# Moving the activations of a decoder layer by 64 bytes against its weights in SBUF

## The chip, the core and the metric

The kernel runs on one core of a Trainium2 chip. The metric is the device time of one execution in microseconds, the median of three runs. The five engines are named as in the profile: PE (TensorE) with its weight loads as PEld, DVE (VectorE), ACT (ScalarE), POOL (GpSimd) and SP (SyncE), which issues nearly all loads.

## The reference, cut to what matters

One decoder layer for 256 tokens of width 1024, all in float32:

```python
h = rmsnorm(x, norm1_g)
proj = h @ w_in                       # q, k/v, gates, MoBA q/k/v, merge gates
y_nsa, y_moba = nsa_attention(...), moba_attention(...)
mixed = g_nsa * (y_nsa @ w_up_nsa) + g_moba * (y_moba @ w_up_moba)
x = x + mixed @ w_out
u = relu(rmsnorm(x, norm2_g) @ w_ff1)
x = x + (u * u) @ w_ff2
return rmsnorm(x, norm_f_g)
```

## The kernel before, in words

Weights come as 60 chunks of up to 128 x 2048 float32 (1 MB), one after the other, through three buffers `raw`. The function `split` (L102) makes two float32r tiles of each chunk: ACT copies it, rounded, to `whi`, and DVE subtracts to give the remainder `wlo`. Activations are split in the same way, into tiles whose names end in h and l. A product of two split operands is three matmuls, high by high, high by low and low by high (`mm3`, L240); nearly every matmul of the kernel goes through the helper `mm` (L237), so the profile shows one line for them and tells them apart by their tiles. Each matmul loads its stationary operand (128 columns, an LDWEIGHTS in the row PEld) and then streams its moving operand. In a name such as `acc<-whi,hTh` the moving operand stands first and the stationary one second.

There are two kinds of these products:

- **Activations stationary, weights moving.** `xstat` (L245) for the input projections with h^T (tiles `hTh`, `hTl`); the products of the attention outputs y^T (`yTh`, `yTl`) with the up-projections (loop at L731); `ff2_mms` (L955) for the second feed-forward product with the squared activations (`sqh`, `sql`); and `seven_mms` (L968), which multiplies six of the sixteen chunks of `ff2` with seven block products instead of eight, its stationary blocks being squared activations or sums of them (`sh`, `sl`, and `sxh`, `sxl` for the sixth), its moving ones weights or differences of weights (`th`, `tl`). The moving operand has 512 columns, except in the first four chunks (384 or 408 columns) and in the last 24 matmuls (256).
- **Weights stationary, activations moving.** `wstat` (L260), with 256 moving columns, for `mixed @ w_out` (tiles `mxh`, `mxl`) and for the first feed-forward product (tiles `h2h`, `h2l`).

The order of the work is written out by hand. `run_slot` (L223) issues the matmuls of one chunk and puts in between, at given shares of the list, the splitting of the chunk after next, the load of a later one, and the steps of the attention. The kernel schedules nothing by itself; the tiles' places in SBUF come from the order in which they are allocated, and unused tiles called `gap...` shift what follows. `act_pair` (L186) makes the pair of tiles that hold h^T first, the mixed activations later, and in the end the sums for the seven products; its argument is the element at which the operand begins in its tile, so the two users can begin at different places of one buffer.

What this case is about is where a partition's bytes of an operand begin, modulo 256. As the built program before has them, in bytes:

| operand | begins at, modulo 256 | past the weights |
|---|---|---|
| `raw`, `whi`, `wlo`, `th`, `tl` | 128 | 0 |
| h^T | 128 | 0 |
| y^T | 128 | 0 |
| squared activations | 128 | 0 |
| sums for the seven products | 128 | 0 |
| mixed activations, `h2h`, `h2l` | 64 | 192 |

All slices of these operands that a matmul takes start a multiple of 256 bytes further, so the table holds for every matmul, with one exception: in the two chunks `kvb` the weights' four blocks have 408 columns, 1632 bytes, so block k begins 1632 k bytes on: 0, 96, 192 and 32 bytes past the first, modulo 256.

Of the kernel before, what the change touches and what calls it, by code (L numbers as in the profile page):

```python
# [8 lines left out]
F32 = mybir.dt.float32  # L9
# [32 lines left out]
def hybrid_layer(ctx: ExitStack, tc: tile.TileContext, firstd, gxd, w, w1c, small, const, gf, out):  # L42
# [8 lines left out]
    ap_ = at_stack.enter_context(tc.tile_pool(name="att", bufs=1))  # L51
# [134 lines left out]
    def act_pair(name, o):  # L186
        return (cp.tile([128, 2048 + e], F32R, name=name + n, tag="act" + n.upper())[:, o:o + 2048]
                .rearrange("p (k q) -> p k q", k=8) for n, e in (("h", 128), ("l", 16)))

    hTh, hTl = act_pair("hT", 16)  # L190

    def h_part(kt):
        x = x0[:, kt, :] if kt < 4 else xT[:, kt, :]
# [266 lines left out]
        act.activation(pcT, tp[:, 0:256], AF.Copy)  # L460


    yTh = {m: ap_.tile([128, 4, 256], F32R, name=f"yTh{m}") for m in "nm"}
    yTl = {m: ap_.tile([128, 4, 256], F32R, name=f"yTl{m}") for m in "nm"}

    PAIRS = [[("n", p, 1), ("n", p, 2)] for p in range(4)] + [
        [("m", p, 0), ("m", p + 1, 0)] for p in (0, 2)]
# [310 lines left out]
    FB = {}  # L778

    def open_ff():  # L780
        at_stack.close()
        FB["p"] = ctx.enter_context(tc.tile_pool(name="ff", bufs=1))
        FB["o"] = ctx.enter_context(tc.tile_pool(name="ps_o", bufs=1, space=PS))
        p = FB["p"]
        p.tile([128, 48], F32, name="gap")
        for n in "hl":
            FB["h2" + n] = (p.tile([128, 2176 if n == "h" else 2096], F32R, name="h2" + n, tag="h2" + n)[:, 48:2096]
                            .rearrange("p (k q) -> p k q", k=8))
        p.tile([128, 80], F32, name="gap2")
        FB["sqh"] = p.tile([128, 32, 256], F32R, name="sqh")  # L790
        FB["sql"] = p.tile([128, 32, 256], F32R, name="sql")
        FB["gfb"] = p.tile([128, 1024], F32, name="gfb")
        FB["x1"] = p.tile([128, 2, 1024], F32, name="x1")
        FB["scr"] = p.tile([128, 1024], F32, name="fscr")
        FB["fst"] = p.tile([128, 24], F32, name="fst")
# [28 lines left out]
    for i in range(4):  # L824
        c = C_WOUT + i
        if i == 0:
            at(0.03, lambda: mix_t(0, 1, bank("yb", "yb")))
            at(0.04, mix_l, 0, 1)
            at(0.29, lambda: mix_t(1, 1, s_tile(1)[:, 0]))
            at(0.3, mix_l, 1, 1)  # L830
            lo_late(0.35, c - 1)
        elif i == 1:
            lo_late(0.03, c - 1)
        split_events(c, (0.0, 0.1), ((9, 9), (0.3, 0.3), (0.3, 0.3), (9, 9))[i])
        for f, a in prev:
            at(0.02, f, *a)
        if i == 1:
            at(0.01, open_ff)
            at(0.9, lambda: act.dma_start(FB["gfb"], gf[None, :].to_broadcast([128, 1024])))
        if i == 3:  # L840
            outs = [acc_tile()[:, 0:256] for _ in range(2)]
            at(0.52, wout_evac, i, outs, (0,))
            run_slot([m for j in range(2)
                      for m in wstat(outs[j], c, j * 128, 8, 256, mxh, mxl)])
            prev = [(wout_evac, (i, outs, (1,)))]
        else:
            mms, outs, _ = two_blocks(c, mxh, mxl, 4 if i == 0 else 8)
            run_slot(mms)
            prev = [(wout_evac, (i, outs))]
# [9 lines left out]
    SS, TT = {}, {}  # L859
# [5 lines left out]

    def s_sums(i, r):
        if not SS:
            FB["p"].tile([128, 40], F32, name="gap3")
            for n, e in (("h", 128), ("l", 16)):
                SS[n] = cp.tile([128, 2048 + e], F32R, name="s" + n, tag="act" + n.upper())  # L870
                SS[n + "x"] = FB["p"].tile([128, 384], F32R, name="sx" + n)
        j = SEVEN.index(i)
        for n in "hl":
            SS[i, n] = (SS[n][:, 16 + 384 * j:400 + 384 * j] if j < 5 else SS[n + "x"])
        S = [FB["scr"][:, 128 * a:128 * a + 128] for a in range(4)]
        A = [[r[:, k, 128 * t:128 * t + 128] for k in range(2)] for t in range(2)]
        for o, x, y, op in ((0, A[1][0], A[1][1], ALU.add), (2, A[0][0], A[1][0], ALU.subtract),
                            (1, S[0], A[0][0], ALU.subtract), (3, A[0][1], S[1], ALU.subtract)):
            dve.tensor_tensor(S[o], x, y, op=op)
# [26 lines left out]
    def ff1_evac(i, outs, whole):  # L906
        r = FB["p"].tile([128, 2, 256], F32, name="ur", bufs=2)
        rf = r.rearrange("p a q -> p (a q)")
        h, l = (FB[n][:, 2 * i:2 * i + 2, :].rearrange("p a q -> p (a q)") for n in ("sqh", "sql"))
        if whole is None:  # L910
            for m in range(2):
                act.activation(r[:, m], outs[m], AF.Relu)
        else:
            act.activation(rf, whole, AF.Relu)
        dve.tensor_tensor(rf, rf, rf, op=ALU.mult)
        act.activation(h, rf, AF.Copy)  # L916
        dve.tensor_tensor(l, rf, h.bitcast(F32), op=ALU.subtract)  # L917
        if i in SEVEN:
            s_sums(i, r)
# [252 lines left out]
```

## Time and profile before

| | |
|---|---|
| median of three runs | 377.09 us (375.64, 377.78, 377.09) |
| span of the profiled execution | 374.1 us |
| PE busy, PEld busy | 365.5 us (98%), 320.9 us (86%) |
| DVE busy, ACT busy | 294.9 us (79%), 219.9 us (59%) |
| matmuls, and as many weight loads | 2388 |
| bytes moved by DMA | 66.89 MB, mean 179 GB/s |
| mean granted TensorE clock | 0.997 |

The page gives no time of the profiled execution other than its span. The three timed runs are 1.5 to 3.7 us above that span, the median 3.0 us; this is what lies around the instructions. The durations of matmuls in the trace overlap, since a matmul's record reaches to the modelled end of its drain. What a matmul takes away from the next is the distance between two starts, and that is what is read below. The stages follow each other in the span: input projections with h^T to about 146 us, with the attention in between; up-projections with y^T from 146 to 173, with the end of the attention in between; `mixed @ w_out` and the first feed-forward product from 173 to 283; the second feed-forward product from 283 to 368; the last sums and stores.

### The profile page before, as it was taken

Reading aid. Unit: us, or ns where it says so; the run is one execution under the profiler, and the core shown is the slowest. Engines: PE = TensorE matmul, PEld = TensorE weight load, DVE = VectorE, ACT = ScalarE, POOL = GpSimd, SP = SyncE. Lnnn points to the kernel's source line nnn. Section 1 sums busy time; section 2 is a strip of 40 time slices with the busy share of each in tenths; the row PEclk is TensorE's granted clock in tenths of the full one; section 3 lists DMA queues with packets and bytes.
Section 4 is the critical chain, followed back from the end, with each engine's and each line's share of the span. In section 5 each row is a group of like instructions: output and inputs, shape, how many; then the busy total and the mean of one; then the engine's idle time right before and its main releaser. Section 6 shows DMA issues by size and latency. Waiting matters only on the chain.

```text
span 374.1 us, 6002 instructions
## 1 busy us (share of the span) xinstructions
PE 365.5 (98%) x2388; PEld 320.9 (86%) x2388; DVE 294.9 (79%) x476; ACT 219.9 (59%) x383; POOL 6.1 (2%) x18
## 2 busy tenths in 40 slices
PE   8999999999999999999999999999999999999993
PEld 7987778878888788778999999999998888888883
DVE  4878888896966869766867688787778879999685
ACT  6966465767747667344455566666664785555412
POOL 2020000000000000000000000000000000000000
PEclk9999999999999999999999999999999999999998
DMA  8996445334533335550675556556655535655202
GB/s 278 366 380 249 142 182 197 112 114 127 189 135 115 112 122 192 155 207 1 223 286 190 185 190 217 156 191 226 209 153 201 203 136 163 231 199 207 100 0 112
DMA packets 10539, 66.89 MB, mean 179 GB/s; under 512 B 1168, under 2 KB 1680, under 8 KB 3216
## 3 DMA queue, kind: packets, MB, share of 16 engines
q1 hardware_dynamic: 10080, 65.61, 50.1%
q10 hardware_dynamic: 432, 0.92, 0.6%
q8 instruction: 18, 0.29, 0.3%
q14 instruction: 9, 0.07, 0.1%
HBM read 65.47 MB, written 1.05 MB: 178 GB/s over the span
## 4 chain that ended last, share of the span: by engine, by line
PE 83%; DVE 7%; ACT 4%; DMA 3%; issue 2%; POOL 1%; SPq 0%; POOLq 0%; ACTq 0%; DVEq 0%
PE acc L238 53%; PE o L238 13%; PE P L238 4%; PE qacc L238 3%; PE yb L238 2%; DVE wlo L116 2%; ACT whi L114 2%; DMA raw<-in_kva_dram 2%; DMA g0x<-in_first_dram 1%; DVE x L988 1%; PE Sa L529 1%; PE Sb L529 1%; PE Sa L238 1%; PE Sb L238 1%; PE tp L319 1%
## 5 line engine op out<-in xcount | busy, mean ns | idle before, releaser
L114 ACT ACTIVATE whi<-raw 128x1024 fp32r<-128x1024 f32 (+3 forms) x124 | 118.4, 984 | 53.2 <-PE acc L238 33.7
L116 DVE TENSOR_TENSOR wlo<-raw,whi 128x1024 fp32r<-128x1024 f32 (+3 forms) x124 | 136.2, 1130 | 13.6 <-ACT whi L114 13.5
L238 PE MATMUL acc<-h2h,whi 128*128 128x256 f32 x256 | 70.7, 276 | 0.0
L238 PE MATMUL acc<-h2l,whi 128*128 128x256 f32 x256 | 70.7, 276 | 0.0
L238 PE MATMUL acc<-h2h,wlo 128*128 128x256 f32 x256 | 70.7, 276 | 0.0
L238 PE MATMUL acc<-whi,hTh 128*128 128x512 f32 (+1 forms) x128 | 51.0, 399 | 0.2 <-DVE kml L338 0.2
L238 PE MATMUL acc<-wlo,hTh 128*128 128x512 f32 (+1 forms) x128 | 50.7, 396 | 0.0
L238 PE MATMUL acc<-whi,hTl 128*128 128x512 f32 (+1 forms) x128 | 49.7, 388 | 0.0
L238 PEld LDWEIGHTS acc<-h2h,whi 128*128 128x128 f32 x256 | 48.0, 188 | 0.0
L238 PEld LDWEIGHTS acc<-h2l,whi 128*128 128x128 f32 x256 | 48.0, 188 | 0.0
L238 PEld LDWEIGHTS acc<-h2h,wlo 128*128 128x128 f32 x256 | 48.0, 188 | 0.0
L238 PE MATMUL o<-whi,sqh 128*128 128x512 f32 (+1 forms) x86 | 33.1, 385 | 0.0
L238 PE MATMUL o<-whi,sql 128*128 128x512 f32 (+1 forms) x86 | 33.0, 384 | 0.0
L238 PE MATMUL o<-wlo,sqh 128*128 128x512 f32 (+1 forms) x86 | 33.0, 384 | 0.0
L238 PEld LDWEIGHTS acc<-whi,hTh 128*128 128x128 f32 x128 | 24.3, 190 | 6.6 <-issue 1.3
L238 PEld LDWEIGHTS acc<-whi,hTl 128*128 128x128 f32 x128 | 24.3, 190 | 4.2
L238 PEld LDWEIGHTS acc<-wlo,hTh 128*128 128x128 f32 x128 | 24.3, 190 | 4.1 <-DVE wlo L116 0.3
L898 ACT ACTIVATE th<-raw 128x1024 fp32r<-128x1024 f32 x12 | 12.7, 1062 | 19.2 <-DVE raw L891 19.2
L917 DVE TENSOR_TENSOR sql<-ur,sqh 128x512 fp32r<-128x512 f32 x16 | 11.1, 693 | 11.2 <-ACT sqh L916 11.2
L238 PEld LDWEIGHTS o<-whi,sql 128*128 128x128 f32 x86 | 16.2, 188 | 3.2
L238 PEld LDWEIGHTS o<-wlo,sqh 128*128 128x128 f32 x86 | 16.2, 188 | 3.2
L238 PEld LDWEIGHTS o<-whi,sqh 128*128 128x128 f32 x86 | 16.1, 188 | 3.1
(318 smaller groups left out, 645.2 us busy)
## 6 DMA issues: line engine op xcount, KB each, us to landing
raw<-in_ff_dram SPq DMA_DIRECT2D x32, 1024.0 KB, 4.9
raw<-in_gm_dram SPq DMA_DIRECT2D x8, 1024.0 KB, 4.8
raw<-in_wout_dram SPq DMA_DIRECT2D x4, 1024.0 KB, 5.1
raw<-in_q_dram SPq DMA_DIRECT2D x2, 1024.0 KB, 5.8
raw<-in_qm_dram SPq DMA_DIRECT2D x2, 1024.0 KB, 7.5
raw<-in_km_dram SPq DMA_DIRECT2D x2, 1024.0 KB, 6.1
raw<-in_vm_dram SPq DMA_DIRECT2D x2, 1024.0 KB, 4.8
raw<-in_upn_dram SPq DMA_DIRECT2D x2, 1024.0 KB, 4.8
```

The costliest lines, as they stand in the source:

```text
L114: act.activation(hi[c][:, a:b], v, AF.Copy)
L116: dve.tensor_tensor(lo[c][:, a:b], v, hi[c][:, a:b].bitcast(F32), op=ALU.subtract)
L238: pe.matmul(o, l, r, start=start, stop=stop, skip_group_check=True)
L319: pe.transpose(tp[:, j * 256 + t * 128:j * 256 + t * 128 + 128], src[:, t, (2 * i + j) * 128:(2 * i + j + 1) * 128], ident)
L529: pe.transpose(S[x][:, j, c:c + 128], P[:, 2 * x + j, c:c + 128], ident)
L898: act.activation(TT["h"][:, v], raw[c][:, v], AF.Copy)
L917: dve.tensor_tensor(l, rf, h.bitcast(F32), op=ALU.subtract)
L988: add = lambda o, v, r: dve.scalar_tensor_tensor(o, v, r, o, op0=ALU.mult, op1=ALU.add)
```

## The change

Four operands begin at another place; the instructions of all engines stay the same and in the same order, with the same shapes, and only addresses differ. h^T and the sums for the seven products begin 64 bytes earlier, at 64 modulo 256, which is 192 past the weights' place. y^T and the squared activations begin 64 bytes later, at 192 modulo 256, which is 64 past it. Everything that lies behind y^T in the attention's pool moves by 512 bytes, a multiple of 256. In the feed-forward pool the tiles behind the squared activations (`gfb`, `x1`, `fscr`, `fst`, `ur`) move by 64 bytes with them. The weights, `th`, `tl`, the mixed activations and `h2` stay.

```diff
-    hTh, hTl = act_pair("hT", 16)
+    hTh, hTl = act_pair("hT", 0)
...
+    ap_.tile([128, 16], F32, name="gapy0")
     yTh = {m: ap_.tile([128, 4, 256], F32R, name=f"yTh{m}") for m in "nm"}
     yTl = {m: ap_.tile([128, 4, 256], F32R, name=f"yTl{m}") for m in "nm"}
+    ap_.tile([128, 112], F32, name="gapy1")
...
-        p.tile([128, 80], F32, name="gap2")
+        p.tile([128, 96], F32, name="gap2")
         FB["sqh"] = p.tile([128, 32, 256], F32R, name="sqh")
...
-            FB["p"].tile([128, 40], F32, name="gap3")
+            FB["p"].tile([128, 8], F32, name="gap3")
...
-            SS[i, n] = (SS[n][:, 16 + 384 * j:400 + 384 * j] if j < 5 else SS[n + "x"])
+            SS[i, n] = (SS[n][:, 384 * j:384 + 384 * j] if j < 5 else SS[n + "x"])
```

## The prediction

> **What bounds the kernel now.** I read the page's table of busy time first, then the busy time by stage, then the chain of waits, and last the timeline of PE alone, since a question about addresses is a question about the distance between the starts of two matmuls. The page and the stages (PE, PEld, DVE, ACT, POOL in order, with instruction counts, then granted clock, DMA share and GB/s):
>
> ```profile
> PE 365.5 (98%) x2388; PEld 320.9 (86%) x2388; DVE 294.9 (79%) x476; ACT 219.9 (59%) x383; POOL 6.1 (2%) x18
> 177.00:283.00 106.00, 106.00 (x936) 106.00 (x936) 83.25 (x124) 63.57 (x90) 0.00 (x0) 1.00 0.60 204
> 283.00:351.00 68.00, 68.00 (x309) 56.51 (x308) 59.25 (x67) 40.73 (x48) 0.00 (x0) 1.00 0.52 186
> ```
>
> From 177 to 351 us PE never rests, at full granted clock (1.00), and nothing else does. In the first feed-forward product (177 to 283) the weight loads are busy all the time too, 106.00 of 106.00 us; in the second (283 to 351) they are busy 56.51 of 68.00. The first is therefore held by loads and matmuls together, the second by the streaming alone. The chain of waits (start, length, what) says the same and gives the distances:
>
> ```profile
> 126.38 9.30 PE acc L238 x40
> ...
> 160.63 1.07 ACT whi L114
> 161.72 2.36 DVE wlo L116 x2
> ...
> 299.05 6.80 PE o L238 x30
> 305.85 2.04 PE P L238 x9
> ```
>
> In the second feed-forward product 30 matmuls take 6.80 us and 9 take 2.04: 226.7 ns each, with 512 columns. In the input projections 40 of the same width take 9.30, which is 0.23 us more than 40 x 226.7 = 9.07. At 161 us the chain leaves PE for a split on ACT and DVE. At the end it is on PE again, as the timeline shows (start, length):
>
> ```profile
> 367.60 0.28 PE L238 MATMUL yb<-whi,sql 128*128 128x256 f32 x1
> 367.86 0.19 ACT L1012 ACTIVATION_READ_ACCUMULATOR fscr<-x 128x1 f32 x1
> 367.91 0.48 DVE L1004 SCALAR_TENSOR_TENSOR x<-yb,fst,x 128x256 f32<-128x256 f32 x1
> ```
>
> DVE takes up the last product as soon as it is there, so whatever each matmul of the last stage gains or loses reaches the end of the span.
>
> **The change part by part.** No instruction is added, removed or moved, so each edit costs whatever it does to the matmuls that read the shifted operand. They are counted from the groups (count, busy us, mean ns of a record, idle time); each row stands for one of three products of a high and low pair:
>
> ```profile
> L238 PE MATMUL acc<-whi,hTh 128*128 128x512 f32 x112 | 45.1, 403 | 0.2 <-DVE kml L338 0.2
> L238 PE MATMUL o<-whi,sqh 128*128 128x512 f32 x82 | 32.0, 390 | 0.0
> L238 PE MATMUL qacc<-whi,hTh 128*128 128x512 f32 x16 | 6.5, 404 | 0.0
> L238 PE MATMUL acc<-whi,yThn 128*128 128x512 f32 x16 | 6.4, 398 | 0.0
> L238 PE MATMUL kvbacc<-whi,hTh 128*128 128x408 f32 x16 | 5.7, 354 | 0.0
> ```
>
> h^T is the stationary operand of 3 x (112 + 16) = 384 matmuls of 512 columns and, by the row of `kvbacc` and one like it with 384 columns, of 96 shorter ones: 480. y^T serves 96 (two tiles, 16 x 3 each). Squared activations and sums serve the second feed-forward product. By the code, eight plain chunks have 24 matmuls of 512 columns each, the last two 18 and 12 of 256 columns, and the six with seven block products 21: 192 + 36 + 126 = 354 of 512 columns and 24 of 256. In all 954 matmuls.
>
> What a shift costs one of them, no row of the trace shows for 512 columns: there the offset between stationary and moving operand is always 0. Three rows come near, and they disagree.
>
> First, 256 columns occur at both offsets. The last 24 matmuls have squared activations stationary at offset 0; the 936 instructions of the stage from 177 us stand at 192.
>
> ```profile
> 364.84 0.28 PE L238 MATMUL o<-whi,sqh 128*128 128x256 f32 x1
> ...
> 366.28 0.28 PE L238 MATMUL yb<-whi,sqh 128*128 128x256 f32 x1
> ```
>
> Twelve starts lie in these 1.44 us, 120.0 ns each. At 192 it is 106.00 / 936 = 113.2 ns. Same shape, 6.7 ns apart, in favour of the shifted place. The loads (PEld) of the two kinds and of the 512 column kind are:
>
> ```profile
> L238 PEld LDWEIGHTS acc<-h2h,whi 128*128 128x128 f32 x256 | 48.0, 188 | 0.0
> L238 PEld LDWEIGHTS o<-whi,sqh 128*128 128x128 f32 x86 | 16.1, 188 | 3.1
> L238 PEld LDWEIGHTS yb<-whi,sqh 128*128 128x128 f32 x4 | 0.8, 192 | 0.0
> ```
>
> A load of the last matmuls takes 192 ns and of the stage at 192 bytes 188. But with 512 columns it takes 188 at offset 0 already, and there PEld has idle time before it (3.1 us in 86), where both kinds with 256 columns have none. So what the shift saves at 256 columns may be a load that a longer matmul hides anyway.
>
> Second, activations are stationary and the offset does vary in the chunk `kvb`, 408 columns: its four blocks begin 0, 96, 192 and 32 bytes past h^T, six matmuls each. These are the first of each six, and the first after them:
>
> ```profile
> 9.97 0.34 PE L238 MATMUL kvbacc<-whi,hTh 128*128 128x408 f32 x1
> ...
> 11.08 0.35 PE L238 MATMUL kvbacc<-whi,hTh 128*128 128x408 f32 x1
> ...
> 12.20 0.35 PE L238 MATMUL kvbacc<-whi,hTh 128*128 128x408 f32 x1
> ...
> 13.32 0.35 PE L238 MATMUL kvbacc<-whi,hTh 128*128 128x408 f32 x1
> ...
> 14.44 0.34 PE L238 MATMUL acc<-whi,hTh 128*128 128x384 f32 x1
> ```
>
> The six at offset 0 take 1.11 us, 185 ns each; at each of the others they take 1.12, or 187. Offset 0 is the cheapest by some 2 ns, and 192, which saved 6.7 with 256 columns, saves nothing here.
>
> Third, 512 columns are not always at 226.7. After a pause of PE the first ones lie further apart:
>
> ```profile
> 95.28 0.40 PE L238 MATMUL acc<-wlo,hTh 128*128 128x512 f32 x1
> ...
> 96.43 0.39 PE L238 MATMUL acc<-whi,hTh 128*128 128x512 f32 x1
> 96.66 0.39 PE L238 MATMUL acc<-wlo,hTh 128*128 128x512 f32 x1
> ...
> 98.02 0.39 PE L238 MATMUL acc<-wlo,hTh 128*128 128x512 f32 x1
> ```
>
> Five take 1.15 us, 230 ns each, the six from 96.66 on 1.36, or 227. Something between load and stream has to fall into step, and the settled step at offset 0 is the shortest that this width shows. All settled distances (113.3, 120.0, 186.7, 226.7) are whole multiples of 6.67 ns: 17, 18, 28 and 34. I read this as a price list: if the settled state of a shifted pair is another one, it differs by 6.67 ns or a multiple.
>
> I take a loss for the forecast, since both rows with activations stationary (second and third) have offset 0 as the best, and the first has the roles exchanged and the load exposed. For 512 columns in the second feed-forward product, where PE runs settled, one step: 354 x 6.67 ns = 2.4 us. For y^T, where ACT and DVE end part of the waits (160 to 164 us above), two thirds of 96 x 6.67 = 0.4. For h^T the row with h^T in it, 2.1 ns: 480 x 2.1 = 1.0; its stage loses part of its time to unsettled starts already. The last 24 are of the width that gained: 24 x 6.67 = 0.2 less. The sum is 2.4 + 0.4 + 1.0 - 0.2 = 3.6 us, and the span goes from 374.1 to 377.7. The median of the timed runs lies 3.0 above the span, so 380.7. The ends of the unknown price are one step off and one step on for all 954, -6.4 and +6.4 us: 370.7 and 383.5; two steps on in the 450 of 512 columns outside the h^T stage would add another 3.0: 386.5.
>
> The writers of the shifted tiles are ACT's copies and DVE's subtractions. They stay the same in number, and each has one duration however its tile's other neighbours are read (shortest, median, longest, ns):
>
> ```profile
> L917 DVE TENSOR_TENSOR sql<-ur,sqh x16: 692/693/694, 204.4 to 285.5; 128x512 fp32r<-128x512 f32 x16
> ```
>
> The sixteen lie within 2 ns. I set the writers at nothing. If each of the 26 whose addresses change in the built program lost 50 ns, that would be 1.3 us of DVE and ACT time, on engines that are busy 59.25 and 40.73 of 68 us beside a full PE.
>
> The Trainium skill ("TensorE: Matmul & The Clock Gate", Part 2, step 1) says that PE has two independent SBUF read ports, one for the streaming operand and one for LDWEIGHTS, and that loading the next weights takes no read bandwidth from the running matmul; by that rule the offset is worth nothing, and the time stays at 377.1. The 120.0 against 113.2 ns at equal shape speak against it for 256 columns, the 185 against 187 ns nearly for it at 408.
>
> **The rivals.** *The step goes down (faster).* Load and stream meet in the same part of SBUF when they begin at equal places, and the meeting costs 6.67 ns per matmul at any width; 512 columns (34 steps, of which 32 are twice the 16 that would be left for 256) are then two steps above their streaming time just as the 256 of the end (18 against 16), and at 192 only one (17). For it: the one clean pair of rows. Against it: `kvb` at 192 and the unchanged 188 ns of a load. If all 954 gain a step: 954 x 6.67 = 6.4 us, 370.7; with a tenth of it lost to splits that then come late, 371.3. It decides from the first settled row of the second feed-forward product: 220 instead of 226.7.
>
> *Nothing changes (same).* With more than 256 columns the load is hidden, and the stream does not care; only the last 24 gain 0.2 us: 376.9. For it: PEld's idle time in that stage and the three equal sixes in `kvb` (1.12 each). A second way to the same total: the two directions oppose each other, y^T and squared activations (+64, 96 + 324 = 420 matmuls) gain a step and h^T and the sums (192, 534) lose one: +0.8 us, 377.9. In the stage at 192 the moving operand lies 64 bytes below the stationary one, which is the relation that y^T and the squared activations get; h^T and the sums get the opposite one.
>
> *Two steps up (slower still).* Like the forecast, at twice its price outside the h^T stage: 380.7 + 3.0 = 383.7, and 386.5 with a full step for h^T.
>
> **How the numbers follow.** A measurement of this kernel can tell about 0.5%, or 1.9 us, from no change. One step up or more: 0.48, of which a small part ends above 386. No net change: 0.22. Step down: 0.30. The likeliest is the first, at 380.7; its own range is 379 to 386. The range to hold 8 in 10 has to reach over to the other sign, to 371, where the step down ends with a little of it lost, and up to 386. Faster by over 0.5% 0.30, within 0.5% 0.22, slower 0.48.
>
> **What would show it.** In the profile of the changed kernel the chain's long pieces of PE from 299 us on: 30 matmuls of 512 columns take 7.00 us at one step up, 6.80 at none, 6.60 at one down. The stage from 177 to 283 us must stay at 113.2 ns, since its operands do not move; if it changes, the cause lies elsewhere. The last 24 matmuls show what the shift does to 256 columns with activations stationary: 113.3 by the exposed load, 120 if the roles and not the offset made the difference. Different distances for the products with squared activations and those with sums, in one chunk, would show that the direction of the shift counts. The prediction is wrong if settled matmuls with 512 columns come out at 220 ns, or stay at 226.7.

## The result and the profile after

The changed kernel takes 379.51 us (median of 11 runs, 378.55 to 381.57) beside 376.85 us for the kernel before (11 runs, 375.36 to 377.78). The ratio is 1.0081, 95% interval 1.0059 to 1.0103: slower by some 2.7 us. The granted clock is 0.997 in both profiles, and the profiled span goes from 374.1 to 377.0 us.

The page's first line, and the two long stages (columns as before):

```profile
PE 368.3 (98%) x2388; PEld 320.5 (85%) x2388; DVE 294.9 (78%) x476; ACT 219.8 (58%) x383; POOL 6.2 (2%) x18
```

```profile
177.60:283.70 106.10, 106.10 (x936) 106.10 (x937) 83.31 (x124) 63.54 (x89) 0.00 (x0) 1.00 0.59 204
283.00:351.00 68.00, 68.00 (x305) 55.26 (x304) 58.52 (x67) 40.59 (x48) 0.00 (x0) 1.00 0.52 188
```

DVE and ACT do the same work in the same time; only PE has grown, by 2.8 us. The stage whose operands stayed still starts a matmul every 106.10 / 936 = 113.4 ns. In 68 us of the second feed-forward product PE now starts 305 matmuls where it started 309. The chain of waits (start, length, what) gives the distances:

```profile
126.74 9.37 PE acc L238 x40
...
177.51 106.25 PE acc L238 x935
...
300.17 7.00 PE o L238 x30
307.17 2.10 PE P L238 x9
```

30 matmuls with squared activations or sums take 7.00 us instead of 6.80, 40 with h^T 9.37 instead of 9.30, and the untouched 935 take 106.25 in both kernels (they begin at 176.72 before). Read from the starts of all of them, the second feed-forward product lasts 2.12 us longer, from its first matmul to the last, and the products with y^T 0.37 us. The remaining 0.4 us of the span had come by 146 us, while h^T is in use; how much of it belongs to the change is taken up below.

A piece of the timeline of PE from the second feed-forward product shows what "7.00" is made of:

```profile
310.27 0.39 PE L238 MATMUL P<-whi,sql 128*128 128x512 f32 x1
310.50 0.40 PE L238 MATMUL o<-whi,sqh 128*128 128x512 f32 x1
310.74 0.39 PE L238 MATMUL o<-wlo,sqh 128*128 128x512 f32 x1
310.97 0.39 PE L238 MATMUL o<-whi,sql 128*128 128x512 f32 x1
311.19 0.39 PE L238 MATMUL o<-whi,sh 128*128 128x512 f32 x1
311.43 0.39 PE L238 MATMUL o<-wlo,sh 128*128 128x512 f32 x1
311.65 0.40 PE L238 MATMUL o<-whi,sl 128*128 128x512 f32 x1
311.89 0.39 PE L238 MATMUL o<-whi,sqh 128*128 128x512 f32 x1
```

The seven distances are 230, 240, 230, 220, 240, 220 and 240 ns in the timeline's rounding; by the trace's whole nanoseconds they are 231, 236, 231, 229, 232, 225 and 236. These lie where squared activations and sums alternate. In the last plain chunks, with squared activations alone, 231 and 236 take turns to the end, and two matmuls together take 466.7 ns; in some earlier ones every distance is 233 or 234, with the same mean. Before, every distance there is 226 or 227, 226.7 in the mean. So a single matmul has no fixed toll; the stream runs in another repeating pattern, which is slower by 6.7 ns per matmul on average. Means given below are over undisturbed matmuls, those that the next one follows without a pause.

### The profile page after: what moved, and what is told of

Same layout as the page of the kernel before. It is cut to its first block, busy times and chain, and to the rows that moved or that the text cites. A ratio compares the mean times of both kernels' runs of the same rounds, so it can differ in the third digit from the quotient of the medians.

```text
span 377.0 us, 6002 instructions
## 1 busy us (share of the span) xinstructions
PE 368.3 (98%) x2388; PEld 320.5 (85%) x2388; DVE 294.9 (78%) x476; ACT 219.8 (58%) x383; POOL 6.2 (2%) x18
## 4 chain that ended last, share of the span: by engine, by line
PE 84%; DVE 6%; ACT 4%; DMA 2%; issue 2%; POOL 1%; POOLq 0%; ACTq 0%; DVEq 0%
PE acc L238 54%; PE o L238 14%; PE P L238 4%; PE qacc L238 3%; PE yb L238 2%; ACT whi L114 2%; DVE wlo L116 2%; DMA raw<-in_kvb_dram 1%; DVE x L990 1%; PE Sa L531 1%; PE Sb L531 1%; PE Sa L238 1%; DMA g0x<-in_first_dram 1%; PE Sb L238 1%; PE tp L319 1%
## 5 line engine op out<-in xcount | busy, mean ns | idle before, releaser
L114 ACT ACTIVATE whi<-raw 128x1024 fp32r<-128x1024 f32 (+3 forms) x124 | 118.4, 983 | 55.1 <-PE acc L238 34.0
```

What stands on the lines that cost most here:

```text
L114: act.activation(hi[c][:, a:b], v, AF.Copy)
```

## The experiments

The prediction's theory has two parts: that the *offset* of the stationary operand against the moving one, modulo 256, sets the distance between starts, and that settled distances are whole steps of 6.67 ns (the *price list*). The rivals at this point: the *place* of an operand by itself counts; the *roles* of weights and activations, and not the offset, set 113.3 against 120.0 ns. Offsets are given as in the table at the top: how far the activations begin past the weights.

**The weights follow.** All weights and their splits move up by 64 bytes. y^T and the squared activations get the place that they have in the changed kernel (192), but at offset 0; h^T and the sums keep 128, which is now offset 192; `mx` and `h2` move with the weights.

```diff
+    gp.tile([128, 16], F32, name="gapw")
+    cp.tile([128, 48], F32, name="gapc")
...
+    ap_.tile([128, 16], F32, name="gapy0")
...
-    mxh, mxl = act_pair("mx", 0)
+    mxh, mxl = act_pair("mx", 16)
...
-        p.tile([128, 80], F32, name="gap2")
+        p.tile([128, 96], F32, name="gap2")
...
```

> The weights, their splits and the differences of weights move 64 bytes up, to 192 modulo 256. Squared activations and y^T stand at 192 as in the changed kernel, so their offset to the weights is 0 again; h^T and the sums stay at 128 as in the kernel before, and are now 192 past the weights, as in the changed kernel; mixed activations and h2 move with the weights. If the offset between the two operands counts: matmuls of 512 columns with squared activations or y^T come back to 226.7 ns, the last 24 to 120.0, those with h^T go to the changed kernel's about 229 (40 in 9.37 us), and the first feed-forward product stays at 113.3; total about 0.8 us over the kernel before, 377.7. If the operand's own place counts (192 is bad, 128 good): 233.3 with squared activations and y^T, 226.7 with h^T; total about 379.0.

Measured: 377.04 us against 376.98, ratio 0.9998 (0.9980 to 1.0015). The chain:

```profile
126.69 9.37 PE acc L241 x40
...
177.13 106.25 PE acc L241 x935
...
299.48 6.81 PE o L241 x30
```

The squared activations stand exactly where they stand in the changed kernel, and 30 matmuls take 6.81 us. h^T has not moved at all; its weights moved away from it. In these pairs the place alone is worth nothing; what counts is the offset between the two operands. In the change the operand was moved without the weights, here the weights without the operand, and the 40 matmuls take the same 9.37 us. The 0.8 us expected on top did not come: the total is the same within its interval.

The transfers that fill the weights' tiles and the splits on ACT and DVE moved along with the weights, so these could be what the matmuls meet. The traces speak against it: in the changed kernel the last transfer has ended 16 us before the last matmul of 512 columns starts, and the last split 8 us before. The final 36 of these matmuls, with neither beside them and DVE at work on other tiles, stand 233.4 ns apart, and 226.7 before.

**Other offsets.** Two kernels put h^T, y^T with the squared activations, and the sums at (64, 128, 0) and at (128, 192, 0) past the weights. The first one's core (the second has 48, 48 and 128 in these lines):

```diff
-    hTh, hTl = act_pair("hT", 16)
+    hTh, hTl = act_pair("hT", 32)
...
+    ap_.tile([128, 32], F32, name="gapy0")
...
-        p.tile([128, 80], F32, name="gap2")
+        p.tile([128, 112], F32, name="gap2")
```

> h^T 64 bytes past the weights (192 in the changed kernel), y^T and squared activations 128 past them (64 in the changed kernel), sums at 0 as before. If any offset other than 0 costs the same step: 233.3 ns for 512 columns with squared activations and y^T, total as the changed kernel, about 379.5. If the cost falls with distance from 0: under 233 at 128. If the direction counts, h^T at +64 loses what y^T and squared activations lost at +64 (40 matmuls in about 9.5 us) instead of the 9.37 that it lost at 192.

> h^T 128 bytes past the weights, y^T and squared activations 192 past them, sums at 0. If the direction counts, squared activations at 192 cost what h^T cost at 192, 229 ns against 226.7, and the second feed-forward product is about 1.5 us shorter than in the changed kernel: total near 378. If every offset costs one step: 233.3, total 379.5 or, with h^T at a step too, up to 381.

Measured: 380.17 us, ratio 1.0085 (1.0054 to 1.0116), and 379.04 us, ratio 1.0059 (1.0031 to 1.0088), both against 376.98. The chains, first of (64, 128, 0), then of (128, 192, 0):

```profile
95.87 9.53 PE acc L238 x40
...
301.35 6.98 PE o L238 x30
```

```profile
96.72 9.52 PE acc L238 x40
...
301.75 6.86 PE o L238 x30
```

40 matmuls with h^T take 9.53 at offset 64 and 9.52 at 128, against 9.37 at 192 and 9.30 at 0. With squared activations the undisturbed distances have a mean of 233 ns at 64, 232.6 at 128 and 229.0 at 192, and the sums, at offset 0 in both kernels, keep 226.8 in the second but take 229.2 among neighbours at 128. The offset's direction counts: 64 and 192 lie equally far from 0 and cost 6.3 and 2.3 ns. As a list of prices for single matmuls the price list falls: 2.3 and 5.9 ns are no multiples of 6.67.

The step itself is still there, in the patterns. At the end of the stage each stream repeats itself: at offset 0 after one matmul (226.7 ns, 34 steps of 6.67), at 64 after two (466.7 ns, 70 steps), at 192 after three (226, 229 and 232 in turn, together 686.7, 103 steps), at 128 after seven (1626.7 ns, 244 steps). Each repeat is a whole number of steps; the single distance is not.

**Weights stationary at offset 0.** The mixed activations and `h2`, which stood at 192, go to 0, with the roles as they were.

```diff
-    mxh, mxl = act_pair("mx", 0)
+    mxh, mxl = act_pair("mx", 16)
...
-            FB["h2" + n] = (p.tile([128, 2176 if n == "h" else 2096], F32R, name="h2" + n, tag="h2" + n)[:, 48:2096]
+            FB["h2" + n] = (p.tile([128, 2176 if n == "h" else 2096], F32R, name="h2" + n, tag="h2" + n)[:, 0:2048]
```

> The other kind of product: mixed activations and h2 (moving, 256 columns, weights stationary) from 192 to 0 past the weights; all else as before. If offset 0 costs 256 columns an exposed load: 120.0 ns instead of 113.3, 960 matmuls x 6.7 = 6.4 us more, total 383. If 113.3 belongs to the roles (weights stationary) and not to the offset: no change, 377.

Measured: 383.39 us against 376.98, ratio 1.0174 (1.0132 to 1.0216). The chain and a window in the stage:

```profile
179.59 112.45 PE acc L238 x935
```

```profile
180.00:290.00 110.00, 110.00 (x919) 110.00 (x919) 81.37 (x123) 63.37 (x89) 0.00 (x0) 1.00 0.57 194
```

935 matmuls take 112.45 us instead of 106.25: 6.2 us more, of the 6.4 between the medians. (The profiled run is the slowest of the four, 385.18 us; it lost another 2.8 us by the end of the stage with h^T, where nothing was moved. The profiles of the other kernels that leave h^T alone reach its last matmul between 0.2 us earlier and 1.1 us later than before. So that stage's length in one profile says little.) The distance is 120 ns, that of the last 24 matmuls of the kernel before, which have the roles exchanged and the same offset. At offset 0 the roles make no difference, and with weights stationary the offset alone makes 6.7 ns. At 192 the roles do count: there the last 24, with activations stationary, take 117.8 ns (in the kernel with squared activations at 192) beside 113.3 with weights stationary.

**The two other offsets for weights stationary.** `mx` at 64 and `h2` at 128 past the weights, by the same two lines with 32 in the first and `[:, 32:2080]` in the second.

> The products with the weights stationary and 256 moving columns: mixed activations 64, h2 128 bytes past the weights, where both were at 192; all else as before. If offset 0 alone is bad here: 113.3 ns for both, no change in the total. If the order of the places counts, 192 being the best as 0 is for the other kind: more than 113.3 for one or both; at 116.7, halfway to 120.0, 960 x 3.4 = 3.2 us more.

Measured: 380.91 us against 376.88, ratio 1.0117 (1.0083 to 1.0150). The chain and a window:

```profile
176.49 111.07 PE acc L238 x935
```

```profile
200.00:280.00 80.00, 80.00 (x676) 80.00 (x676) 60.37 (x94) 48.73 (x69) 0.00 (x0) 1.00 0.57 190
```

The window holds `h2` at 128: 80.00 / 676 = 118.3 ns. The mean of the undisturbed ones is 118.7, and 117.4 for `mx` at 64. So all three other offsets tried are worse for this kind, and the kernel before has the best of the four there too.

**Offsets of 32 bytes.** h^T at 224, y^T at 96, squared activations at 32, sums at 0: perhaps a fine step finds something below 226.7.

```diff
-    hTh, hTl = act_pair("hT", 16)
+    hTh, hTl = act_pair("hT", 8)
...
+    ap_.tile([128, 24], F32, name="gapy0")
...
-        p.tile([128, 80], F32, name="gap2")
+        p.tile([128, 88], F32, name="gap2")
```

> Offsets between the multiples of 64: squared activations 32 bytes past the weights, y^T 96, h^T 224; sums at 0. If places count in pieces of 64 bytes: 32 costs 512 columns what 0 or 64 cost, 226.7 or 233.3 ns, and 224 what 192 or 0 cost. If an offset just off 0 is better than 0, a settled distance under 226.7 appears, and the kernel beats both. By the chunks with 408 columns, where 32 and 96 cost what 192 cost, I expect none: 229 to 233 for all three, total 378 to 380.

Measured: 382.83 us against 376.62, ratio 1.0166 (1.0094 to 1.0238), its runs far apart (379.63 to 385.04). The chain:

```profile
96.92 9.53 PE acc L238 x40
...
302.60 6.99 PE o L238 x30
```

All three are as bad as 64: means of 233.0, 233.8 and 233.2 ns, in the order of the line above. No offset tried beats 0 for 512 columns with activations stationary. The total lies above the 378 to 380 that was expected, and the distances do not explain all of it: of the 5.3 us by which the profiled span grew, 2.1 lie in the second feed-forward product, 0.4 in the products with y^T and 2.8 in the stage with h^T, where 384 matmuls at some 4 ns each make only 1.6.

**Which of the three matmuls pays.** Of the three matmuls of a product two have the high half stationary and one the low half. One kernel moves the low half of the squared activations by 64 bytes, another the high half. Three theories: each matmul pays for the offset of its *own pair*; or a *load* disturbs the matmul that streams beside it, the one before it; or what costs is the *change of place* from one load to the next. The first kernel's core (a smaller gap further on keeps the sums at 0):

```diff
         FB["sqh"] = p.tile([128, 32, 256], F32R, name="sqh")
+        p.tile([128, 16], F32, name="gapl")
         FB["sql"] = p.tile([128, 32, 256], F32R, name="sql")
```

> Only the low halves of the squared activations stand 64 bytes past the weights; the high halves and all else as before. In each three (high by high, high by low, low by high) the weight load for the third runs while the second streams. If a load disturbs the matmul that streams during it: the distance from the second matmul's start to the third's grows, the other two stay near 226.7. If the pair of operands of one matmul counts: the third grows. If each shifted load costs the same 6.67 ns on average: 228.9 over all three, 30 matmuls in 6.87 us.

> The counterpart of the run with the low half moved: the high halves of the squared activations stand 64 bytes past the weights, the low halves at 0. If a matmul is stretched by the offset between its own two operands: the first and the second of each three take 233 ns or more, the third stays near 226.7. If it is the load of the next stationary operand: the first (beside it the second's load, high) and the third (beside it the next first's load, high) grow and the second (beside it the low half's load) stays. If it is the change of place from one load to the next: the distances at both changes grow, in this run as in the other.

Measured, one run each: 378.20 us beside 376.88, and 378.24 beside 376.62. The chain of waits, first with the low half moved, then with the high half:

```profile
299.67 6.93 PE o L238 x30
```

```profile
299.69 6.99 PE o L238 x30
```

By position, in the order in which they are issued (high by high, high by low, low by high), the mean distances are 228.3, 228.9 and 235.5 ns with the low half moved, and 233.8, 231.5 and 234.4 with the high half moved. With the low half moved the third position pays most, its own pair, which speaks against the load as I had put it. With the high half moved the third has its own pair at offset 0 and pays 234.4 all the same, which speaks against the own pair. The first pays 233.8 there, with no change of place to the next load, which speaks against the third theory. And the two do not add: the stage grows by 1.32 us with the low half and 2.08 us with the high half, but 2.12 with both (in the change, which moves the sums too). None of the simple theories holds. With the low half moved the settled pattern repeats after three matmuls (693.3 ns, 104 steps), with the high half only after six (1400.0 ns, 210 steps), and with both after two, which does not follow the three positions at all: what a matmul pays depends on the matmuls before it too.

**Shorter loads.** If load and stream meet, a load of fewer columns meets less. Two kernels load 64 of the 128 columns in three chunks, one with the squared activations at offset 64 and one at offset 0; a third has 32 columns at offsets 0, 64, 128 and 192 in four chunks and 64 columns at 64 and 192 in two, by slices that begin later in the same tiles. All three leave out output rows of those chunks. The lines that the first two share:

```diff
+        m = 64 if i in (5, 7, 9) else 128
...
-            lh, ll = (FB[a][:, kt, t * 128:(t + 1) * 128] for a in ("sqh", "sql"))
+            lh, ll = (FB[a][:, kt, t * 128:t * 128 + m] for a in ("sqh", "sql"))
...
-            r += mm3(ops[p][:, 0:n], lh, ll, hi[c][:, a:a + n], lo[c][:, a:a + n],
+            r += mm3(ops[p][0:m, 0:n], lh, ll, hi[c][:, a:a + n], lo[c][:, a:a + n],
```

> Squared activations 64 bytes past the weights as in the changed kernel, all else as before; and in the chunks 5, 7 and 9 of the second feed-forward product the matmuls use 64 stationary columns instead of 128, so that half of those products' output rows are left out. 512 moving columns stream as before. If what stretches a matmul is the weight load that runs beside it: half the load gives about half of what lies over the bare streaming, taken as 32 steps or 213.3 ns: 233.3 becomes about 223. If the stream itself is slower at this place, whatever is loaded: 233.3.

> As the run before, with the squared activations at offset 0. If the weight load is the cause: 226.7 becomes about 220. If the 226.7 is the stream's own pace: 226.7 stays.

> All tiles stand as in the kernel before. In six plain chunks of the second feed-forward product the matmuls take fewer stationary columns, from a chosen place in the tile, so that most of those chunks' output rows are left out or wrong: chunk 3 takes 32 columns at offset 0, chunk 5 32 at 64, chunk 7 32 at 128, chunk 9 32 at 192, chunk 11 64 at 64, chunk 13 64 at 192. A load of 32 columns reads 128 bytes of each partition, two pieces of 64. If the beginning of the load sets the pace, the distances by offset stay as with full loads: 226.7, 233.3, 232.5 and 229. If the stretch comes from meetings spread over the load, a load that is over after a quarter leaves the stream nearly bare: 215 to 220 at every offset. If the pace is the stream's own and the load only sets its phase: one value for all with 32 columns, whatever the offset, between 226 and 234.

Measured, one run each: 378.98 us beside 376.88; 376.10 beside 376.88; 376.56 beside 376.55. The chain at offset 0, with full loads in the first row and half loads in 24 of the 30 in the second:

```profile
299.06 6.80 PE o L238 x30
309.26 6.88 PE o L238 x30
```

At offset 64, half loads:

```profile
310.93 6.98 PE o L238 x30
```

With 32 columns, the loads of one group (count, busy us, mean ns), and the chain at offsets 0, 64, 128 and 192:

```profile
L238 PEld LDWEIGHTS o<-whi,sqh 128*32 128x32 f32 x32 | 3.5, 108 | 3.6
```

```profile
299.09 6.92 PE o L238 x30
309.45 6.91 PE o L238 x30
319.76 6.89 PE o L238 x30
330.07 6.91 PE o L238 x30
```

A load of 32 columns takes 108 ns instead of 188, and at offset 0 the shorter load parts the matmuls instead of bringing them closer: 230.0 ns with half loads (6.88 - 6.80 = 0.08 us over 24 matmuls, 3.3 ns each above 226.7). With 32 columns all four offsets give nearly one value, 231.7, 231.1, 230.6 and 231.1 ns; with 64 columns it is 232.8 at offset 64 and 228.4 at 192. So with little load beside it the stream runs near 231 ns at all four offsets. A full load at offset 0 goes with 226.7, below that pace, and a full load at offset 64 with 233. The picture with which the experiment began, a clean stream to which a badly placed load adds collisions, falls. What these runs do not separate: a matmul with fewer stationary columns also fills fewer output rows, so the shorter load and the narrower matmul were tested together.

## Why the prediction came out right, point by point

- **The sign and the sum.** Forecast 380.7, measured 379.51; the span was to grow by 3.6 us and grew by 2.9 in the profile. The direction was argued from two rows with activations stationary. The experiments bear out the conclusion, that for 512 columns of that kind offset 0 is the best of those tried, but not the rows: one of them (`kvb`, below) does not carry over, and the other shows no offset but 0. So the sign, given 0.48, was in part luck.
- **Second feed-forward product, +2.4 us.** Measured +2.12. The pointer (30 matmuls in 7.00 us) was hit to the digit. At 64 the price of one step is right on average: two matmuls take 70 steps instead of 68. The rule behind it, that the settled distance of a shifted pair differs by 6.67 ns or a multiple, failed: at 192 the mean price is 2.3 ns, at 128 5.9. That the largest part of the change went to 64 and not to 192 was luck for this term. The sums, at 192 but set among matmuls with squared activations at 64, pay 232.3 ns there, and 229.1 where they alone are shifted, with the weights moved. In the kernel with squared activations at 192 and sums at 0, one step for each of the 300 shifted matmuls of 512 columns would be 2.0 us, and the stage lost 0.62.
- **y^T, +0.4 us.** Measured +0.37.
- **h^T, +1.0 us.** Over-sized, and its row was the wrong one. 40 matmuls went from 9.30 to 9.37 us, 1.75 ns each; over 384 of 512 columns this is 0.7 us at most, and the mean over undisturbed ones alone, 228.9 to 229.7 ns, gives 0.3. (It is so little because before, too, the matmuls after a pause of PE lie mostly 228 to 236 ns apart until they settle at 226.7.) The profile cannot say better: the last matmul with h^T begins 0.43 us later than before, but also 0.41 later in the kernel in which only the low half of the squared activations moved. The 2.1 ns came from `kvb`, and that chunk has its own prices: after the change its blocks stand at 192, 96, 0 and 160, and

```profile
12.76 0.35 PE L238 MATMUL kvbacc<-whi,hTh 128*128 128x408 f32 x1
...
13.87 0.35 PE L238 MATMUL kvbacc<-whi,hTh 128*128 128x408 f32 x1
...
15.00 0.33 PE L238 MATMUL acc<-whi,hTh 128*128 128x384 f32 x1
```

  the six at offset 0 again take 1.11 us and those at 160 1.13. The mean over all undisturbed matmuls of 408 columns is 186.2 ns before and after: all offsets moved and nothing was lost there. In the kernel with h^T at 64, where no block stands at 0, the two sixes at offset 128 take 1.10 and 1.11, no more than those at 0, and the mean over all is 184.6. So the price of that chunk is its own, and the row from which the sign was partly argued did not hold what I read in it.
- **The last 24 matmuls, -0.2 us.** Measured -0.05:

```profile
367.80 0.28 PE L238 MATMUL o<-whi,sqh 128*128 128x256 f32 x1
...
369.21 0.28 PE L238 MATMUL yb<-whi,sqh 128*128 128x256 f32 x1
```

  Twelve starts lie in 1.41 us, by the trace's nanoseconds 117.8 ns each: neither the 113.3 that an exposed load was to give nor the 120 of the roles. The row of 120.0 against 113.2 ns had been set aside because the roles are exchanged there and the load is exposed. The kernel with weights stationary at 0 shows that the offset alone makes this difference when weights are stationary; with activations stationary it makes 2.2 ns at 64 and at 192. Setting the row aside for 512 columns was right in its outcome: the offset that is worst for 256 columns, 0, is the best for 512.
- **Writers, +0.** Right: DVE and ACT are busy for 294.9 and 219.8 us, as before.
- **Around the span, 3.0 us.** Sized from one profile with a short span. In most of the timed runs the time lies 1.8 us above the span of the same run, in both kernels (median spans 374.9 and 377.6). This did no harm, since the forecast's base held the same surplus: of the 1.2 us between 380.7 and 379.5, 0.9 is the growth (3.6 forecast, 2.7 in the medians) and 0.2 the median of before (377.09 then, 376.85 now).
- **The rivals.** *Step down* fell at its own pointer: 226.7 went to 233, not 220. *Nothing changes* fell by the ratio's interval. *Directions oppose* was half right, and it is this that I had not priced: they do differ, 6.3 ns at 64 and 2.3 at 192, but both cost. *Two steps up* did not occur. The Trainium skill ("TensorE: Matmul & The Clock Gate", Part 2, step 1) has independent read ports for the two operands, and says that a load takes no read bandwidth from the running matmul; taken as the prediction took it, this gives one time for every offset. 106.25 against 112.45 us for the same 935 matmuls is against it.

What stays open is why. The runs show that the offset between the operands decides, that with 32 stationary columns the pace is near 231 ns at every offset tried, that the stream settles into patterns of whole steps, and that what a matmul pays depends on those before it. They do not show what load and stream share, where the step comes from, nor why 512 columns are best at 0 and 256 worst there. They also do not test the modulus: offsets of 0 to 224 bytes were tried, and that 256 brings the pattern back is only read off the slices of each operand, which begin multiples of 256 apart. One pair contradicts any table by offset alone: activations stationary at 64 and weights stationary at 192 have the stationary operand 64 bytes past the moving one, at equal shapes, and settle at 117.8 and 113.3 ns.

## What to carry to other kernels

Where PE runs one matmul and one weight load after another without rest, write down for each product where its two operands begin modulo 256, and read the distance between starts: equal shapes with unequal distances are worth a padding tile. Measure each shape and role by itself, since the best offset of one (0, at 512 columns with activations stationary) was the worst of another (0, at 256 with weights stationary), and the rows of 408 columns did not carry over. The loss was 1 to 6 per cent of those matmuls' time and shows in no busy share: PE stood at 97 or 98% in every kernel here, and only the distances, or the count of matmuls per window, give it away.

## What the runs showed of the hardware

Mean distance between the starts of undisturbed matmuls, ns, by how far the activations begin past the weights:

| | 0 | 32 | 64 | 128 | 192 |
|---|---|---|---|---|---|
| 512 columns, activations stationary (squared activations) | 226.7 | 233.2 | 233.0 | 232.6 | 229.0 |
| 256 columns, weights stationary | 120.0 | | 117.4 | 118.7 | 113.3 |
| 256 columns, activations stationary (last 24) | 120.0 | 118.7 | 117.8 | 118.4 | 117.8 |

In a settled stream of 512 columns a single distance need not be a multiple of 6.67 ns, but the repeat of the pattern is one: 34 steps per matmul at offset 0, 70 in two at 32 and at 64, 103 in three at 192, 244 in seven at 128.

Not expected was that the stream is slower with a shorter load: at offset 0 and 512 columns, 226.7 ns with loads of 128 columns (188 ns each), 230.0 with 64 and 231.7 with 32 (108 ns each). Nor that a matmul is the slower for another's place: with only the high half of the squared activations moved, those with the unmoved low half stationary take 234.4 ns.
